# Half of the first mixer's v by seven products of quarters, and the token tiles moved to the front of the constant pool

## The chip, the cores and the metric

The kernel runs on one core of a Trainium2 chip. The metric is the device time of one execution in microseconds (us). The kernel before took 1327.69 us, the median of three runs from 1327.13 to 1328.07.

## The reference

A trunk of two layers works on 512 tokens of width 1024. Layer 0 mixes tokens with a gated MLP (mixer A), layer 1 with a gated linear recurrence (mixer B); after each mixer comes a gated feed-forward part with a short causal convolution (conv_ffn). The change touches mixer A, and within it v:

```
def mixer_a(h, w_in, v_gain, w_s, b_s, w_out):
    z = jax.nn.gelu(h @ w_in)
    u, v = jnp.split(z, 2, axis=-1)
    v = rms_norm(v, v_gain)
    v = v.reshape(bsz, s // CHUNK, CHUNK, A_GROUPS, A_GDIM)
    ws = jnp.tril(w_s).astype(v.dtype)
    sv = jnp.einsum("gts,bcsgd->bctgd", ws, v) + b_s.T.astype(v.dtype)[:, :, None]
    y = u * sv.reshape(bsz, s, A_WIDTH)
    return y @ w_out
```

Here h is the RMS-normed input (512 x 1024), w_in is 1024 x 4096, and u and v are 512 x 2048 each. All inputs and outputs are float32.

## The kernel before

**Numbers in two parts.** Each float32 operand of a product is split into a float32r part hi (a copy by ACT, ScalarE) and a rest lo (a subtraction on DVE, VectorE). A product of two operands is three matmuls: hi by hi, and the two mixed ones. `split` (L95) does this for weights that `load` (L103) brings in on SP's DMA queue; raw, hi and lo tiles rotate in the pool wp through three buffers each.

**Tokens.** `xall` holds the residual stream with the 512 tokens along the free axis, in 8 rows of 512 for the 1024 channels. `norm_input` (L210) writes gain times x in two parts, `xh[k]` and `xl[k]`, 8 tiles of 128 x 512 each. The factor 1/rms of a token, `rc`, is applied to the results instead of to x: as a scale per partition in v, where tokens lie on the partitions, and elsewhere through `rbc`, which is rc spread over all partitions. `norm_stat` (L230) forms sums of squares with eight tiny matmuls (`st`), DVE makes `ms` of them, and a power on POOL (GpSimd) makes `rc` (L226). `norm_spread` (L236) multiplies an identity by the two parts of rc on DVE (tiles `dg`) and sums these over partitions with two matmuls into the bank `rb`, which ACT copies to rbc.

**The constant pool.** `vt` (all gains, biases and convolution taps, 536 columns), `xall`, `xh`, `xl` and, further down, `acc` and `rbc` are declared in this order (L138 to L204), and the pool lays its tiles out in the order of declaration. In the built program the pool begins at byte 16512 of a partition, which is 258 x 64, and vt with it; vt takes 536 x 4 = 2144 bytes, 33.5 x 64, so every tile from xall to xl[7] starts 32 bytes past a multiple of 64. All tiles of the pools wp, yp and y, which hold the other matmul operands, start on a multiple of 64.

**The order of stages.** v in four blocks of 512 features (L359 to L390); u in four blocks, with the spatial product `gate_spatial` (matmuls `sv`) of the block before hooked in between; the output projection `ao`; conv_ffn(0); mixer B (`bx`, gates `gt`, `bg`, projection `bo`); conv_ffn(1). In v the token parts are the stationary operand and the weights (512 columns) the moving one. In u, bx, bg and the up-projections `f` the weights are stationary and xh or xl, 512 columns, moves. In ao, bo, gt and the down-projections xh and xl are not used.

**v, block by block.** Block 0 (`first_chunk`, L344) loads tokens and weights together. Each block has four chunks `kc` of two channel rows each, a chunk being 2 x 4 x 3 matmuls of 512 columns into four PSUM banks; at the end ACT takes each bank through gelu with the scale rc (`vr`) and a square with a running sum (`junk`). norm_stat stands behind block 0, norm_spread in front of chunk 2 of block 1. Afterwards the gain `rv` comes from the sums by the same power on POOL, and `vh` and `vl` (ACT, DVE) are the two parts of the normed v.

**Seven products.** conv_ffn's down-projections use a scheme that multiplies two 2 x 2 arrangements of quarters with seven products in place of eight (`PRODUCTS`, L467; `weight_sums`, L470; `seven`, L510). weight_sums loads three quarters and copies with three DMAs on SP, adds the fourth quarter to two of them with one accumulating DMA on POOL's queue (L475), and leaves two more sums to DVE. seven keeps seven PSUM banks, one for each product; each product of a pair of channel rows is 2 x 3 matmuls of 256 columns.

**Who sets the order.** A scheduler orders the instructions of each engine when the program is built; parts written under `tc.high_priority` come as early as it thinks they can run. On the chip each engine and each DMA queue works through its own list in that order.

Of the kernel before, what the change touches and what calls it, by code (L numbers as in the profile page):

```python
# [44 lines left out]
def trunk(ctx: ExitStack, tc: tile.TileContext, xT, vecs, a_w_in, a_w_sT, a_b_s, a_w_out,  # L45
# [7 lines left out]
    def psum(name="ps"):  # L53
        return pp.tile([P, S], F32, tag="ps", name=name)
# [16 lines left out]
    def keep(tag, name, dt=F32):  # L71
        return phase["yp"].tile([P, S], dt, tag=tag, name=name)
# [18 lines left out]
    def small(n, name):  # L91
        return const.tile([P, n], F32, name=name)
# [10 lines left out]
    def load(shape, parts, name):  # L103
        raw = wp.tile(shape, F32, tag="raw", name=f"{name}r")
        for sl, src in parts:
            nc.sync.dma_start(sl(raw), src)
        return split(raw, shape, name)
# [27 lines left out]
        return f  # L135


    vt = const.tile([P, NV], F32, name="vt")  # L138
    xall = const.tile([P, KD, S], F32, name="xall")
    xs = [xall[:, k, :] for k in range(KD)]  # L140
    xh = [const.tile([P, S], F32R, name=f"xh{k}") for k in range(KD)]
    xl = [const.tile([P, S], F32R, name=f"xl{k}") for k in range(KD)]
    xparts = list(zip(xh, xl))
    g0 = const.tile([P, KD], F32, name="g0")
    nc.scalar.dma_start(g0, vecs[:, _COLS["norm_mix"]:_COLS["norm_mix"] + KD])

    def load_x(k):
        nc.sync.dma_start(xs[k], xT[k * P:(k + 1) * P, :])

    mixer = enter(("yp", 24), ("wk", 6), ("bs", 1))  # L150
    bs = phase["bs"].tile([P, AG, P], F32, name="bs")


# [46 lines left out]
        nc.vector.tensor_scalar(c4, u, LRU_C / 2, None, op0=ALU.mult)  # L200


    acc = const.tile([P, S], F32, name="acc")
    rbc = const.tile([P, S], F32, name="rbc")  # L204
    rc = small(NC, "rc")
    ms = small(NC, "ms")
    rch = const.tile([P, NC], F32R, name="rch")
# [61 lines left out]
    def project_out(kt, w, acts, name):  # L269
# [64 lines left out]
            dg = stat(1)  # L334
        leave(1, dg)

    tiny = small(1, "tiny")
    nc.vector.memset(tiny, 0.0)
    nc.scalar.activation(tiny, tiny, AF.Gelu_apprx_tanh)
# [19 lines left out]
    for fb in range(4):  # L359
        pss = [psum(f"v{c}") for c in range(NC)]  # L360
        for kc in range(KD // 2):
            c0 = AW + fb * 512
            if fb == 0:
                hi, lo = first_chunk(kc, wv[:, 2 * kc:2 * kc + 2, c0:c0 + 512])
            else:
                hi, lo = load([P, 2, 512], [(lambda t: t, wv[:, 2 * kc:2 * kc + 2, c0:c0 + 512])], f"av{fb}{kc}")
            if fb == 1 and kc == 2:
                norm_spread()
            last = kc == KD // 2 - 1
            order = [(k, c) for c in range(NC) for k in range(2)] if last else [(k, c) for k in range(2) for c in range(NC)]  # L370
            for k, c in order:
                kk = 2 * kc + k
                ts = slice(c * P, (c + 1) * P)
                nc.tensor.matmul(pss[c], xh[kk][:, ts], hi[:, k, :], start=kk == 0, stop=False)  # L374
                nc.tensor.matmul(pss[c], xh[kk][:, ts], lo[:, k, :], start=False, stop=False)  # L375
                nc.tensor.matmul(pss[c], xl[kk][:, ts], hi[:, k, :], start=False, stop=kk == KD - 1)  # L376
            if fb == 0:
                square(2 * kc)
# [86 lines left out]
    HS = S // 2  # L465

    PRODUCTS = ((1, 0, 0, 0), (2, 0, 2, 1), (4, 0, 1, 6), (6, 1, 2, 5), (7, 1, 0, 4), (5, 1, 1, 3), (3, 1, 3, 2))  # L467


    def weight_sums(src, name):  # L470
        raw = wp.tile([P, 5, 256], F32, tag="raw", name=f"{name}r")
        for k, n, to in ((1, 0, raw[:, 1:5:3]), (0, 1, raw[:, 0:4:3])):
            nc.sync.dma_start(to, src[:, k, n:n + 1].broadcast_to([P, 2, 256]))
        nc.sync.dma_start(raw[:, 2], src[:, 1, 1])
        nc.gpsimd.dma_start(raw[:, 3:5], src[:, 0, 0:1].broadcast_to([P, 2, 256]), accum_op=ALU.add)  # L475
        sums = phase["sm"].tile([P, 2, 256], F32, tag="sm", name=f"{name}s")

        def part(n, t):
            return tuple(wp.tile([P, n, 256], F32R, tag=g, name=f"{name}{t}{g}", padded_shape=[P, 4, 256]) for g in ("hi", "lo"))

        def fill(hi, lo, src):
            nc.scalar.copy(hi, src)
            nc.vector.tensor_tensor(lo, src, hi.bitcast(F32), op=ALU.subtract)

        with tc.high_priority(HIGH):
            ah, al = part(3, "a")
            fill(ah, al, raw[:, 0:3])
            nc.vector.tensor_tensor(sums[:, 0], raw[:, 0], raw[:, 4], op=ALU.add)
            nc.vector.tensor_tensor(sums[:, 1], raw[:, 2], sums[:, 0], op=ALU.add)
            bh, bl = part(4, "b")  # L490
            fill(bh[:, 0:2], bl[:, 0:2], raw[:, 3:5])
            fill(bh[:, 2:4], bl[:, 2:4], sums)
        return (ah, al), (bh, bl)


    def input_sums(raw, dst):
        nc.vector.tensor_tensor(raw[:, 3:5], raw[:, 0:3:2], raw[:, 7:8].broadcast_to([P, 2, HS]), op=ALU.subtract)  # L497
        nc.vector.tensor_tensor(raw[:, 5], raw[:, 3], raw[:, 2], op=ALU.add)
        nc.vector.tensor_tensor(raw[:, 6], raw[:, 5], raw[:, 1], op=ALU.subtract)  # L499
        hi, lo = dst[:, :, 0:HS], dst[:, :, HS:S]  # L500
        nc.scalar.copy(hi, raw[:, 0:7])  # L501
        nc.vector.tensor_tensor(lo, raw[:, 0:7], hi.bitcast(F32), op=ALU.subtract)  # L502


    def places(raw):
        return raw[:, 0:8:7], raw[:, 1:3]

    def halves(t):
        return t.rearrange("p (h t) -> p h t", h=2)


    def seven(pairs, weight, name):
        banks = {p[0]: psum(f"{name}m{p[0]}").rearrange("p (j t) -> p j t", j=2) for p in PRODUCTS}
        for n, (q, x) in enumerate(pairs):
            parts = weight_sums(weight(q), f"{name}{q}")
            first, last = n == 0, n == len(pairs) - 1
            for b, part, w, i in PRODUCTS:
                hi, lo = parts[part]
                for j in range(2):
                    js = slice(j * P, (j + 1) * P)  # L520
                    for m, (wt, xt) in enumerate(((lo, x[:, i, 0:HS]), (hi, x[:, i, 0:HS]), (hi, x[:, i, HS:S]))):
                        nc.tensor.matmul(banks[b][:, j], wt[:, w, js], xt, start=first and j == 0 and m == 0,  # L522
                                         stop=last and j == 1 and m == 2, skip_group_check=True)
        return banks

    def conv_ffn(l, gain_name, gain_off, chunks):
        stack = enter(("y", 6), ("yr", 1), ("sm", 1), ("wk", 8))
# [240 lines left out]
```

## Time and profile before

| | us |
|---|---|
| median of 3 runs | 1327.69 |
| the profiled execution | 1328.25 |
| its span, first to last instruction | 1326.5 |
| TensorE busy | 1316.4 (99%) |
| VectorE (DVE) busy | 935.2 (71%) |
| ScalarE (ACT) busy | 600.6 (45%) |
| GpSimd (POOL) busy | 54.3 (4%) |

The profile is of one execution. A busy share of 99% tells that matmuls follow each other without a break, and not that each is as short as it could be, since their recorded spans overlap: a matmul of 512 columns is recorded with 0.39 to 0.40 us while the next begins 0.23 us later. The distance from one start to the next is what to read.

### The profile page before, as it was taken

The page shows a single profiled execution, that of the slowest core. Times are in us where ns is not written, and L with a number is a line of the kernel's source. Part 1 is how long each engine was busy: PE and PEld are TensorE (multiplying, and loading weights), DVE is VectorE, ACT ScalarE, POOL GpSimd, SP SyncE. Part 2 cuts the span into 40 slices and gives each one's busy share as a digit, 9 for nine tenths or more (in the row PEclk, how much of TensorE's full clock was granted, in tenths as well). Part 3 has the DMA queues.
Part 4 walks back from the last instruction along what each step waited for, and adds up shares of the span by engine and source line. Part 5 has one row for each costly group of instructions (what it writes and reads, how often), then busy time and mean ns, then how long its engine had stood idle before and what let it go on. Part 6 is the DMA issues. An engine that isn't in the chain of part 4 may idle for free.

```text
span 1326.5 us, 17029 instructions
## 1 busy us (share of the span) xinstructions
PE 1316.4 (99%) x6510; PEld 1103.5 (83%) x6510; DVE 935.2 (71%) x1336; ACT 600.6 (45%) x809; POOL 54.3 (4%) x56
## 2 busy tenths in 40 slices
PE   9999999999999999999999999999999999999997
PEld 7888888888888898888997888888888899888886
DVE  7227776446777877878987799954687788576735
ACT  6456333333444443444554669633344444343432
POOL 1000000000000120001200000000000012000000
PEclk9999999999999999999999999999999999999999
DMA  6333222232223574225752323233222357322221
GB/s 231 96 95 111 81 80 80 95 97 95 95 96 94 124 188 130 89 92 130 178 137 96 96 80 95 96 111 96 84 91 96 111 135 182 113 95 96 96 80 64
DMA packets 121105, 143.47 MB, mean 108 GB/s; under 512 B 7616, under 2 KB 95168, under 8 KB 121024
## 3 DMA queue, kind: packets, MB, share of 16 engines
q1 hardware_dynamic: 111088, 132.95, 31.5%
q0 software_dynamic: 9792, 9.44, 4.7%
q8 instruction: 51, 0.84, 0.3%
q14 instruction: 30, 0.25, 0.1%
q10 hardware_dynamic: 144, 0.00, 0.0%
HBM read 140.26 MB, written 2.10 MB: 107 GB/s over the span
## 4 chain that ended last, share of the span: by engine, by line
PE 99%; issue 1%; DVE 0%; DVEq 0%; POOLq 0%; POOL 0%
PE f L111 14%; PE f L112 14%; PE f L113 14%; PE v L374 2%; PE d000m L522 2%; PE d001m L522 2%; PE v L375 2%; PE u L111 2%; PE d101m L522 2%; PE d061m L522 2%; PE d100m L522 2%; PE d060m L522 2%; PE u L113 2%; PE u L112 2%; PE v L376 2%; PE aop L111 2%
## 5 line engine op out<-in xcount | busy, mean ns | idle before, releaser
L458 DVE SCALAR_TENSOR_TENSOR cv<-up,vt,cv 128x511 f32<-128x511 f32 x192 | 135.8, 745 | 0.7
L545 DVE TENSOR_TENSOR up<-f,rbc 128x512 f32<-128x512 f32 x96 | 63.7, 686 | 35.6 <-PE f L113 33.2
L456 ACT ACTIVATE cv<-up,vt 128x512 f32<-128x512 f32 x96 | 70.7, 804 | 0.5 <-DVE up L545 0.5
L561 ACT ACTIVATE cv<-cv 128x512 f32<-128x512 f32 x48 | 30.3, 632 | 34.4 <-DVE cv L458 34.3
L502 DVE TENSOR_TENSOR y<-yr,y 128x1792 fp32r<-128x1792 f32 x18 | 36.5, 2025 | 11.8 <-ACT y L501 11.8
L501 ACT CAST y<-yr 128x1792 fp32r<-128x1792 f32 x18 | 30.4, 1691 | 14.3 <-DVE yr L499 14.3
L226 POOL TENSOR_TENSOR rc<-ms,mhalf 128x4 f32<-128x4 f32 (+1 forms) x6 | 5.5, 912 | 665.2 <-DVE ms L225 665.2
L434 DVE SCALAR_TENSOR_TENSOR sv<-sv,vt,bs 128x256 f32<-128x256 f32 x32 | 15.0, 478 | 19.1 <-PE sv L431 19.1
L211 ACT ACTIVATE xh<-xall,vt 128x512 fp32r<-128x512 f32 x24 | 17.1, 717 | 20.3 <-DVE xall L263 15.8
L220 ACT ACTIVATE sq<-xall 128x512 f32<-128x512 f32 (+1 forms) x37 | 21.5, 586 | 9.8 <-DVE xall L275 9.8
L563 DVE TENSOR_TENSOR yr<-cv 128x512 f32<-128x512 f32 x36 | 24.7, 688 | 1.7
L458 DVE SCALAR_TENSOR_TENSOR xb<-xr,vt,xb 128x511 f32<-128x511 f32 (+2 forms) x36 | 25.5, 744 | 0.1
L221 DVE TENSOR_TENSOR acc<-acc,sq 128x512 f32<-128x512 f32 (+1 forms) x37 | 23.8, 642 | 2.0 <-ACT sq L220 1.9
L212 DVE SCALAR_TENSOR_TENSOR xl<-xall,vt,xh 128x512 fp32r<-128x512 f32 x24 | 17.8, 747 | 3.4 <-ACT xh L211 3.2
L430 PE MATMUL sv<-ws,vh 128*128 128x256 f32 x64 | 15.4, 324 | 0.0
L436 DVE SCALAR_TENSOR_TENSOR sv<-sv,vt 128x256 f32<-128x256 f32 x32 | 15.0, 479 | 0.4
L567 ACT CAST y<-cv 128x512 fp32r<-128x512 f32 x12 | 7.3, 617 | 16.1 <-DVE cv L565 16.1
L431 PE MATMUL sv<-ws,vl 128*128 128x128 f32 x64 | 14.2, 223 | 0.0
L698 DVE TENSOR_TENSOR_SCAN hs<-riyh,sq 128x512 f32<-128x512 f32 x12 | 14.0, 1207 | 0.0
L86 ACT ACT_TABLE_LOAD x10 | 12.8, 1283 | 0.1
L497 DVE TENSOR_TENSOR yr<-yr 128x512 f32<-128x512 f32 x18 | 12.5, 692 | 0.6
L431 PEld LDWEIGHTS sv<-ws,vl 128*128 128x128 f32 x64 | 12.3, 192 | 0.5
(2631 smaller groups left out, 4505.7 us busy)
## 6 DMA issues: line engine op xcount, KB each, us to landing
xall<-xT SPq DMA_DIRECT2D x8, 256.0 KB, 5.3
outT<-o SPq DMA_DIRECT2D x8, 256.0 KB, 2.2
av00raw<-a_w_in SPq DMA_DIRECT2D x2, 256.0 KB, 4.3
av01raw<-a_w_in SPq DMA_DIRECT2D x2, 256.0 KB, 5.6
av02raw<-a_w_in SPq DMA_DIRECT2D x2, 256.0 KB, 5.8
av03raw<-a_w_in SPq DMA_DIRECT2D x2, 256.0 KB, 4.8
bs<-a_b_s SPq DMA_DIRECT2D x1, 512.0 KB, 5.9
av10r<-a_w_in SPq DMA_DIRECT2D x1, 512.0 KB, 6.0
```

The source lines that it names most:

```text
L111: nc.tensor.matmul(ps, wh, xh, start=first, stop=False)
L112: nc.tensor.matmul(ps, wh, xl, start=False, stop=False)
L113: nc.tensor.matmul(ps, wl, xh, start=False, stop=last)
L374: nc.tensor.matmul(pss[c], xh[kk][:, ts], hi[:, k, :], start=kk == 0, stop=False)
L375: nc.tensor.matmul(pss[c], xh[kk][:, ts], lo[:, k, :], start=False, stop=False)
L456: nc.scalar.activation(dst, src, AF.Identity, scale=col(wname, woff + last * wstep), bias=col(cname, coff))
L458: nc.vector.scalar_tensor_tensor(dst[:, i:], src[:, :S - i], col(wname, woff + (last - i) * wstep), dst[:, i:], op0=ALU.mult, op1=ALU.add)
L501: nc.scalar.copy(hi, raw[:, 0:7])
L502: nc.vector.tensor_tensor(lo, raw[:, 0:7], hi.bitcast(F32), op=ALU.subtract)
L522: nc.tensor.matmul(banks[b][:, j], wt[:, w, js], xt, start=first and j == 0 and m == 0, stop=last and j == 1 and m == 2, skip_group_check= ...
L545: nc.vector.tensor_tensor(upt, pss[2 * half + j], rbc, op=ALU.mult)
L561: nc.scalar.activation(ts[0], ts[0], AF.Gelu_apprx_tanh)
```

## The change

Two edits.

1. In the constant pool the tiles are declared in the order xall, xh, xl, acc, rbc, vt. In the built program xall then begins at byte 16512, and every xh, xl, acc and rbc on a multiple of 64. The pool's size and the places of the other pools are the same.
2. Blocks 2 and 3 of v go by seven products. During block 1 `v_sums` builds, for each pair q of channel rows, the four sums of token halves that the scheme needs (ACT scales two rows into `xg`, four half-width operations on DVE, and the two parts `xq` of the results by ACT and DVE). In blocks 2 and 3 the weights come by `weight_sums`; the seven banks are combined by two copies on ACT and eleven operations on DVE into vr, and gelu and square then read vr. The mixer's work pool (`wk`) has five tiles in place of six; the sixth becomes the tile of weight sums (`sm`).

```diff
-    vt = const.tile([P, NV], F32, name="vt")
     xall = const.tile([P, KD, S], F32, name="xall")
...
     xparts = list(zip(xh, xl))
+    acc = const.tile([P, S], F32, name="acc")
+    rbc = const.tile([P, S], F32, name="rbc")
+    vt = const.tile([P, NV], F32, name="vt")
...
-    mixer = enter(("yp", 24), ("wk", 6), ("bs", 1))
+    mixer = enter(("yp", 24), ("sm", 1), ("wk", 5), ("bs", 1))
...
+    def v_sums(q):
+        g = []
+        for k in (2 * q, 2 * q + 1):
+            t = work(f"xg{k}")
+            nc.scalar.activation(t, xs[k], AF.Copy, scale=g0[:, k:k + 1])
+            g.append((t[:, 0:HS], t[:, HS:S]))
+        (p_, q_), (r_, s_) = g
+        a, b = work(f"xa{q}"), work(f"xb{q}")
+        nc.vector.tensor_tensor(a[:, 0:HS], p_, q_, op=ALU.subtract)
+        nc.vector.tensor_tensor(a[:, HS:S], s_, q_, op=ALU.subtract)
+        nc.vector.tensor_tensor(b[:, 0:HS], a[:, 0:HS], s_, op=ALU.add)
+        nc.vector.tensor_tensor(b[:, HS:S], b[:, 0:HS], r_, op=ALU.subtract)
+        parts = [to_parts(t, f"xq{q}{i}") for i, t in enumerate((a, b))]
...
-    for fb in range(4):
+    for fb in range(2):
...
             if fb == 0:
                 square(2 * kc)
                 square(2 * kc + 1)
+            else:
+                v_sums(kc)
...
+    for fb in range(2, 4):
+        banks = seven_banks(f"v{fb}")
+        for q in range(KD // 2):
+            parts = weight_sums(wv4[:, 2 * q:2 * q + 2, fb], f"av{fb}{q}")
+            for b, part, w, i in PRODUCTS:
+                wh, wl = (t[:, w] for t in parts[part])
+                sh, sl = xsums[q][i]
+                for j in range(2):
+                    js = slice(j * P, (j + 1) * P)
+                    for n, (st, mv) in enumerate(((sh, wh), (sl, wh), (sh, wl))):
+                        nc.tensor.matmul(banks[b][:, j], st[:, js], mv, start=q == 0 and j == 0 and n == 0,
+                                         stop=q == KD // 2 - 1 and j == 1 and n == 2, skip_group_check=True)
+        for c in range(NC):
+            vraw[c, fb] = keep("yl", f"vr{c}{fb}")
+        e1, e5, u2, u3 = (work(f"v{fb}{t}").rearrange("p (j t) -> p j t", j=2) for t in ("e1", "e5", "u2", "u3"))
...
+        for c in range(NC):
+            v_gelu(c, fb, vraw[c, fb])
```

`weight_sums` and `PRODUCTS` are those of the down-projections, moved up in the file unchanged.

How the instructions stand on three engines around block 1 of v. On POOL, around the power that makes rc (`ms` is its input, `av20r` the raw weights of the first pair of block 2), before:

```order
L188 TENSOR_TENSOR lu_121<-ebase_118,nabs_119 128x12
L226 TENSOR_TENSOR rc_128<-ms_129,mhalf_116 128x4
L409 AFFINE_SELECT wsm_844<-wsr_842 128x256
L409 AFFINE_SELECT wsm_849<-wsr_842 128x256
L409 AFFINE_SELECT wsm_854<-wsr_842 128x256
```

and in the change:

```order
L191 TENSOR_TENSOR lu_126<-ebase_123,nabs_124 128x12
L351 DMA av20r_575<-a_w_in 128x2x256
L227 TENSOR_TENSOR rc_131<-ms_132,mhalf_121 128x4
L351 DMA av21r_635<-a_w_in 128x2x256
L351 DMA av22r_695<-a_w_in 128x2x256
```

The first of eight accumulating DMAs now stands ahead of the power; it waits for two of the three loads of av20r on SP's queue.

On DVE, from the parts of rc (rch, rcl) to the tiles dg that norm_spread's matmuls read, before:

```order
L238 TENSOR_TENSOR rcl_131<-rc_128,rch_130 128x4
L100 TENSOR_TENSOR av12l_410<-av12r_407,av12h_409 128x1024
L242 TENSOR_TENSOR dg_416<-ident_111,rch_130 128x512
L242 TENSOR_TENSOR dg_419<-ident_111,rcl_131 128x512
L100 TENSOR_TENSOR av13l_450<-av13r_447,av13h_449 128x1024
```

and in the change, the last twelve of eighteen rows that stand from rch on:

```order
L439 TENSOR_TENSOR xa0_384<-xg1_382,xg0_380 128x256
L440 TENSOR_TENSOR xb0_385<-xa0_384,xg1_382 128x256
L441 TENSOR_TENSOR xb0_385<-xb0_385,xg1_382 128x256
L255 TENSOR_TENSOR xq00l_391<-xa0_384,xq00h_390 128x512
L255 TENSOR_TENSOR xq01l_395<-xb0_385,xq01h_394 128x512
L438 TENSOR_TENSOR xa1_432<-xg2_428 128x256
L439 TENSOR_TENSOR xa1_432<-xg3_430,xg2_428 128x256
L440 TENSOR_TENSOR xb1_433<-xa1_432,xg3_430 128x256
L359 TENSOR_TENSOR av20alo_582<-av20r_575,av20ahi_581 128x768
L441 TENSOR_TENSOR xb1_433<-xb1_433,xg3_430 128x256
L255 TENSOR_TENSOR xq10l_439<-xa1_432,xq10h_438 128x512
L243 TENSOR_TENSOR dg_455<-ident_116,rch_133 128x512
```

Chunk 3's split (av13l), the sums of two pairs and a split of block 2 now stand ahead of the first dg; the second dg follows one row later, behind xq11l.

On TensorE, where the two matmuls of norm_spread (`rb`) stand in block 1, before:

```order
L376 MATMUL v3_346<-av11h_379,xl3_77 128x512
L246 MATMUL rb_415<-dg_416,ones_109 128x512
L246 MATMUL rb_415<-dg_419,ones_109 128x512
L374 MATMUL v0_343<-av12h_409,xh4_70 128x512
L375 MATMUL v0_343<-av12l_410,xh4_70 128x512
```

and in the change:

```order
L470 MATMUL v1_347<-av12l_449,xh5_70 128x512
L247 MATMUL rb_454<-dg_455,ones_114 128x512
L471 MATMUL v1_347<-av12h_448,xl5_78 128x512
L469 MATMUL v2_348<-av12h_448,xh5_70 128x512
L470 MATMUL v2_348<-av12l_449,xh5_70 128x512
L471 MATMUL v2_348<-av12h_448,xl5_78 128x512
L247 MATMUL rb_454<-dg_458,ones_114 128x512
```

They stood in front of chunk 2's 24 matmuls and now stand behind the 17th and the 21st of them.

## Rows read from the trace of the kernel before

**Rows 1.** The page: the chain that ended last, shares of the span by engine.
```profile
PE 99%; issue 1%; DVE 0%; DVEq 0%; POOLq 0%; POOL 0%
```

**Rows 2.** Waits of TensorE, the longest of three: total us, times, longest us.
```profile
PE rb L298 <- DVE dg L291: 1.5, 1, 1.5
```

**Rows 3.** Timeline of TensorE, u to the gates' matmuls, one engine load: start us, us.
```profile
733.64 0.40 PE L113 MATMUL bx<-xh,bx20l 128*128 128x512 f32 x1
...
734.58 0.40 PE L111 MATMUL gt<-xb0h,gw0h 128*128 128x512 f32 x1
...
736.87 0.39 PE L112 MATMUL gt<-xb1l,gw0h 128*128 128x512 f32 x1
```

**Rows 4.** Timeline of TensorE: first matmul of five up blocks, of what follows; same for bop.
```profile
509.08 0.40 PE L111 MATMUL f<-xh,fu070h 128*128 128x512 f32 x1
...
621.53 0.28 PE L522 MATMUL d060m<-y,d0606alo 128*128 128x256 f32 x1
...
851.73 0.40 PE L111 MATMUL bop<-by0h,bow00h 128*128 128x512 f32 x1
...
917.03 0.40 PE L111 MATMUL f<-xh,fu100h 128*128 128x512 f32 x1
```

**Rows 5.** Timeline of TensorE: first matmul of v's block 2, and of u.
```profile
52.65 0.40 PE L374 MATMUL v<-av20h,xh 128*128 128x512 f32 x1
...
97.45 0.40 PE L111 MATMUL u<-xh,au00h 128*128 128x512 f32 x1
```

**Rows 6.** The chain in order of time: seven products of a half, 252 matmuls of 256 columns.
```profile
1075.97 30.23 PE d100m L522 x252
```

**Rows 7.** DMA issues, window 5 to 40 us: size, us to landing.
```profile
vt<-vecs SPq DMA_DIRECT2D x1, 268.0 KB, 5.2
```

**Rows 8.** Timelines of SP and POOL: the load after av11l, and the power that gives rc.
```profile
28.40 0.37 SPq L106 DMA_DIRECT2D av20r<-a_w_in  x1
30.12 1.01 POOL L226 TENSOR_TENSOR rc<-ms,mhalf 128x4 f32<-128x4 f32 x1 [6.85 <-DVE ms L225]
```

**Rows 9.** Timelines of SP and POOL: two sums loaded and added to, d0609r and d0011r.
```profile
619.36 0.88 SPq L473 DMA_DIRECT2D d0609r<-f_w_down  x2
...
623.98 1.20 POOL L475 DMA_DIRECT2D d0609r<-f_w_down  x1 [8.71 <-DMA d0609r<-f_w_down]
...
468.34 0.97 SPq L473 DMA_DIRECT2D d0011r<-f_w_down  x2
...
474.30 1.20 POOL L475 DMA_DIRECT2D d0011r<-f_w_down  x1 [4.18 <-DMA d0011r<-f_w_down]
```

**Rows 10.** Timeline of ACT after rc, in v's second block.
```profile
31.16 1.27 ACT L386 ACTIVATE vr<-v,rc 128x512 f32<-128x512 f32 x2 [1.03 <-POOL rc L226]
...
35.91 1.05 ACT L99 CAST av13h<-av13r 128x1024 fp32r<-128x1024 f32 x1
```

**Rows 11.** Timeline of DVE in the seven products: 256, 768 and 512 elements.
```profile
470.70 0.42 DVE L489 TENSOR_TENSOR d0005s<-d0005r,d0005s 128x256 f32<-128x256 f32 x1
471.04 0.95 DVE L483 TENSOR_TENSOR d0005alo<-d0005r,d0005ahi 128x768 fp32r<-128x768 f32 x1
471.91 0.68 DVE L483 TENSOR_TENSOR d0005blo<-d0005r,d0005bhi 128x512 fp32r<-128x512 f32 x1
```

**Rows 12.** Timeline of TensorE: start of v's second block; spreading of rc.
```profile
29.70 0.48 PE L374 MATMUL v<-av10h,xh 128*128 128x512 f32 x1
...
40.98 0.63 PE L246 MATMUL rb<-dg,ones 128*128 128x512 f32 x2
```

**Rows 13.** Timeline of TensorE from the start: ten bfloat16 matmuls of 512 columns, first of v.
```profile
1.26 4.45 PE L158 MATMUL warm<-warm 128*128 128x512 bf16 x10 [1.26 <-DVE warm L155]
...
5.57 1.73 PE L374 MATMUL v<-av00hi,xh 128*128 128x512 f32 x4
```

**Rows 14.** Timeline of DVE after v: first of u's banks, first sum of sv.
```profile
117.82 1.88 DVE L448 TENSOR_TENSOR u<-u,rbc 128x512 f32<-128x512 f32 x3
...
126.17 0.48 DVE L434 SCALAR_TENSOR_TENSOR sv<-sv,vt,bs 128x256 f32<-128x256 f32 x1 [3.56 <-PE sv L431]
```

More of the change, by code (lines that the diff above doesn't have):

```diff
@@ L200, in log_sigmoid @@
         nc.vector.tensor_scalar(c4, u, LRU_C / 2, None, op0=ALU.mult)
-    acc = const.tile([P, S], F32, name="acc")
-    rbc = const.tile([P, S], F32, name="rbc")
     rc = small(NC, "rc")
@@ L335, in project_out, with weight_sums, part, fill @@
         leave(1, dg)
+    HS = S // 2
+    PRODUCTS = ((1, 0, 0, 0), (2, 0, 2, 1), (4, 0, 1, 6), (6, 1, 2, 5), (7, 1, 0, 4), (5, 1, 1, 3), (3, 1, 3, 2))
+    def weight_sums(src, name):
+        raw = wp.tile([P, 5, 256], F32, tag="raw", name=f"{name}r")
+        for k, n, to in ((1, 0, raw[:, 1:5:3]), (0, 1, raw[:, 0:4:3])):
+            nc.sync.dma_start(to, src[:, k, n:n + 1].broadcast_to([P, 2, 256]))
+        nc.sync.dma_start(raw[:, 2], src[:, 1, 1])
+        nc.gpsimd.dma_start(raw[:, 3:5], src[:, 0, 0:1].broadcast_to([P, 2, 256]), accum_op=ALU.add)
+        sums = phase["sm"].tile([P, 2, 256], F32, tag="sm", name=f"{name}s")
+        def part(n, t):
+            return tuple(wp.tile([P, n, 256], F32R, tag=g, name=f"{name}{t}{g}", padded_shape=[P, 4, 256]) for g in ("hi", "lo"))
+        def fill(hi, lo, src):
+            nc.scalar.copy(hi, src)
+            nc.vector.tensor_tensor(lo, src, hi.bitcast(F32), op=ALU.subtract)
+        with tc.high_priority(HIGH):
+            ah, al = part(3, "a")
+            fill(ah, al, raw[:, 0:3])
+            nc.vector.tensor_tensor(sums[:, 0], raw[:, 0], raw[:, 4], op=ALU.add)
+            nc.vector.tensor_tensor(sums[:, 1], raw[:, 2], sums[:, 0], op=ALU.add)
+            bh, bl = part(4, "b")
+            fill(bh[:, 0:2], bl[:, 0:2], raw[:, 3:5])
+            fill(bh[:, 2:4], bl[:, 2:4], sums)
+        return (ah, al), (bh, bl)
@@ new lines, in input_sums, with places @@
+    def input_sums(raw, dst):
+        nc.vector.tensor_tensor(raw[:, 3:5], raw[:, 0:3:2], raw[:, 7:8].broadcast_to([P, 2, HS]), op=ALU.subtract)
+        nc.vector.tensor_tensor(raw[:, 5], raw[:, 3], raw[:, 2], op=ALU.add)
+        nc.vector.tensor_tensor(raw[:, 6], raw[:, 5], raw[:, 1], op=ALU.subtract)
+        hi, lo = dst[:, :, 0:HS], dst[:, :, HS:S]
+        nc.scalar.copy(hi, raw[:, 0:7])
+        nc.vector.tensor_tensor(lo, raw[:, 0:7], hi.bitcast(F32), op=ALU.subtract)
+    def places(raw):
+        return raw[:, 0:8:7], raw[:, 1:3]
@@ new lines, in halves, with seven_banks, seven @@
+    def halves(t):
+        return t.rearrange("p (h t) -> p h t", h=2)
+    def seven_banks(name):
+        return {p[0]: psum(f"{name}m{p[0]}").rearrange("p (j t) -> p j t", j=2) for p in PRODUCTS}
+    def seven(pairs, weight, name):
+        banks = seven_banks(name)
+        for n, (q, x) in enumerate(pairs):
+            parts = weight_sums(weight(q), f"{name}{q}")
+            first, last = n == 0, n == len(pairs) - 1
+            for b, part, w, i in PRODUCTS:
+                hi, lo = parts[part]
+                for j in range(2):
+                    js = slice(j * P, (j + 1) * P)
+                    for m, (wt, xt) in enumerate(((lo, x[:, i, 0:HS]), (hi, x[:, i, 0:HS]), (hi, x[:, i, HS:S]))):
+                        nc.tensor.matmul(banks[b][:, j], wt[:, w, js], xt, start=first and j == 0 and m == 0,
+                                         stop=last and j == 1 and m == 2, skip_group_check=True)
+        return banks
@@ L357, in first_chunk, with v_gelu @@
         return hi, lo
-    for fb in range(4):
+    xsums = []
+    def v_sums(q):
[11 more added lines that the diff above has]
+        parts = [to_parts(t, f"xq{q}{i}") for i, t in enumerate((a, b))]
+        t0, t1 = slice(0, HS), slice(HS, S)
+        k = 2 * q
+        xsums.append([(h[:, t], l[:, t]) for h, l, t in (
+            (xh[k], xl[k], t0), (xh[k + 1], xl[k + 1], t0), (xh[k + 1], xl[k + 1], t1),
+            (*parts[0], t0), (*parts[0], t1), (*parts[1], t0), (*parts[1], t1))])
+    def v_gelu(c, fb, src):
+        v = vraw[c, fb]
+        nc.scalar.activation(v, src, AF.Gelu_apprx_tanh, scale=rc[:, c:c + 1])
+        junk = work("junk")
+        i = c * 4 + fb
+        nc.scalar.activation(junk, v, AF.Square, accum_out=vsum[:, i:i + 1])
+    for fb in range(2):
         pss = [psum(f"v{c}") for c in range(NC)]
         for kc in range(KD // 2):
[L362 to L366, printed above, removed]
+            src = wv[:, 2 * kc:2 * kc + 2, AW + fb * 512:AW + (fb + 1) * 512]
+            hi, lo = load([P, 2, 512], [(lambda t: t, src)], f"av{fb}{kc}") if fb else first_chunk(kc, src)
             if fb == 1 and kc == 2:
@@ L460, in conv @@
                 op0=ALU.mult, op1=ALU.add)
[L465 to L493, printed above, removed]
@@ L496, in input_sums @@
[L496 to L506, printed above, removed]
@@ L508, in halves @@
[L508 to L524, printed above, removed]
```

27 lines of the change are left out of this document (21 added, 6 removed).

## The prediction

> **What bounds the kernel now.** I read the chain that ended last first. It is TensorE for 99% [rows 1], and the longest wait of that engine is 1.5 us near the end [rows 2]. So in this kernel a microsecond is won or lost only where matmuls start closer together or further apart, or where TensorE newly waits. The next view is therefore TensorE's timeline, read from start to start, since the recorded spans overlap.
>
> There the same shape has two spacings. Five up blocks `f`, 20 x 24 = 480 matmuls of 512 columns, lie between 509.08 and 621.53: 112.45/480 = 0.2343 us each. The 288 of `bop` lie between 851.73 and 917.03: 65.30/288 = 0.2267 [rows 4]. Both have the same tile sizes and the same order of three matmuls. The difference is not one of the stretch either: inside one engine load, the last four matmuls of bx take (734.58 - 733.64)/4 = 0.235, and the ten of gt behind them (736.87 - 734.58)/10 = 0.229 [rows 3]. What sets the two kinds apart is the moving operand. In f, bx, bg and u it is xh or xl, which starts 32 bytes past a multiple of 64, because vt stands ahead of it: its 268.0 KB are 128 rows of 2144 bytes [rows 7], 33.5 times 64. In bop and gt it starts on a multiple. 7.5 ns are 18 columns at 2.4 GHz, close to the 16 float32 values that 64 bytes hold, as if one more piece were read. That is a reading of two numbers, not a proof; no row shows xh at another place.
>
> In v, xh and xl are the stationary operand. From the start of block 2 to u, 44.80 us, lie 192 matmuls: 0.2333 each [rows 5].
>
> **The change, part by part.**
>
> *Starts on 64 bytes, moving operand.* u has 384 such matmuls, the two conv_ffn 2304, bx and bg 288 each: 3264. At 7.5 ns each that is **-24.6 us**. Bounds: nothing, if the spacing has another cause, and these 24.6. I take the whole, since every stage that reads xh has the long spacing and those with other operands the short one. All of it lies on the path as long as the splits of weights keep up; in these stages they stand 6 us or more ahead of their matmuls, and each group of 24 shortens by 0.18 us.
>
> *The same, stationary operand.* Blocks 0 and 1 of v keep 192 matmuls. 0.2333 - 0.2267 = 6.6 ns each: **-1.3 us**, bounds 0 and 1.3.
>
> *Seven products in blocks 2 and 3.* 44.8 us go [rows 5]. In their place come 2 blocks x 4 pairs x 42 = 336 matmuls of 256 columns. 252 of that kind took 30.23 us in the down-projection [rows 6], 0.120 each: 40.3 us. The difference is **-4.5 us**. The weight sums need more loads and more DVE work than a plain split; the down-projection runs two halves of six such pairs with no pause, so eight pairs in a row are covered once the first is ready.
>
> *POOL's queue, and a new wait.* Before, rc is ready at 30.12 + 1.01 = 31.1 [rows 8], and the two matmuls `rb`, at 40.98, find dg done [rows 12]. Now the accumulating DMA of av20r stands ahead of the power, and POOL takes its list in order. That DMA waits for loads that stand behind av11l's on SP, where av20r was issued at 28.40 [rows 8]. In the down-projection POOL began on such a DMA 4.6 us after the first of the two loads was issued (619.36 to 623.98) or 6.0 (468.34 to 474.30), and spent 1.20 on it [rows 9]. So 28.4 + 4.6 + 1.2 = 34.2, and the power ends at 35.2; the ends are 34.3 (loads 0.9 us faster than in the faster of these two) and 36.6.
>
> What is behind rc: ACT has four gelus and four squares, which took from 31.16 to 35.91, and then 1.05 for av13h [rows 10]. DVE waits for that with av13l (1024 wide, about 1.2 by the 768-wide row), and then has the eight small sums of two pairs at 0.42 (256 wide), four parts of 0.68 (512 wide), and av20alo at 0.95 (768 wide) [rows 11], each pair interleaved with ACT's xg and xq. Adding these in the order shown for DVE I get the first dg 13.6 us behind rc, 48.8, and the second at about 50.
>
> TensorE: block 1 starts at 29.70 [rows 12], less 0.5 for the shorter spacing in block 0: 29.2. The first rb now stands behind 65 of its matmuls, 65 x 0.2267 = 14.7: TensorE is there at 43.9. It waits from 43.9 to 48.8: **+4.9 us**, with 3.9 and 6.3 as the ends of rc's range. The four matmuls between the two rb cover most of what the second is late.
>
> *Smaller waits.* In block 2 the bank of the fifth product is free only when the last gelu of block 1 has read it, which now stands behind av21's splits on ACT: +0.35 (0 to 1). The entry into the first seven products of conv_ffn and the rb of bx have thin leads already, and TensorE now comes sooner: +0.4 (0 to 1). u's banks are emptied from 117.82, before the sums of the first `sv` at 126.17 [rows 14]. Now gelu of v's last block reads results that DVE combines first, so the parts of v come some 5.5 us later against TensorE, which was covered by u's first block but for about 0.1. ACT's and DVE's other new work (11 operations a block for the combination) lies beside matmuls.
>
> *Sum:* -24.6 - 1.3 - 4.5 + 4.9 + 0.35 + 0.4 + 0.1 = -24.65. The profiled execution took 1328.25, 0.56 above the median of 1327.69. 1328.25 - 24.65 - 0.56 = **1303.0 us**.
>
> **Rivals.**
>
> *C, the clock falls after the pause.* At the program's start TensorE, idle before, takes 4.45 us for ten matmuls and 1.73 for the first four of v, about 0.43 each; that is 512 columns at the lower level of 1.2 GHz. It is at the upper level some 5.3 us after its first matmul [rows 13]. A pause of nearly 5 us, longer than any in the trace of before, could bring that back: half of 5.3 is lost, about 2.5 us, so 1305.5. Against it: nothing in the rows tells how long a pause may be. The Trainium skill ("TensorE: Matmul & The Clock Gate", What's actually happening) has the idle engine at 1.2 GHz and releases it only after sustained activity; the first matmuls of this trace agree with the second half, and no row of before shows a fall in mid-kernel.
>
> *D, no pause.* The loads land early, or POOL is not held at the accumulating DMA, and ACT and DVE interleave better than I added up: 1303.0 - 4.9 = 1298.1. Against it, POOL shows the wait for such loads as its own idle time [rows 9].
>
> *A, starts on 64 bytes bring nothing.* The spacing would belong to the stage (which pools it reads, how weights follow each other), not to the address. Then -4.5 + 5.75 = +1.25: 1328.9. Against it, the change from 0.235 to 0.229 inside one engine load, where only the operands differ [rows 3]. The Trainium skill speaks for this rival ("TensorE: Matmul & The Clock Gate", Wait — 56ns, not 53.3ns?): it has the distance between matmuls as the number of columns over 2.4 GHz plus a fixed 2.5 ns, about 216 ns for 512 columns, and the address does not occur. By that rule alone both kinds would be equal and the first two terms nothing; the trace, with 226.7 and 234.3 for 512 columns, disagrees on the equality.
>
> *B, slower.* The wait at rb in block 1 outweighs what is won. Place: POOL's queue, av20r's DMA ahead of rc's power. Price: a microsecond for each that rc comes late, plus the clock of C. While starts on 64 bytes count, the wait and what follows from it would have to cost over 30.4 us, which no row comes near. If they don't, the point is lower: 4.5 to make it slower at all, 4.5 + 2.7 = 7.2 to be seen as slower. The wait of 4.9, the small ones of 0.85 and C's 2.5 make 8.25, so +3.75: 1331.4.
>
> **How the numbers follow.** My forecast 0.50, C 0.25, D 0.08, A 0.07, B 0.06; 0.04 is left for what I have not seen, half of it inside the gain. The range goes from 1297.5, a little under D, to 1309.0, which takes in C with the wait at its long end and the small ones at 1 us each, or a fifth of the gain on starts missing: some 0.83 of the chance. A measurement of this kernel can tell about 0.2%, 2.7 us, from no change. The forecast, C, D and half of the rest are faster by more than that, 0.86; A and the other half lie within it or near, 0.08; B is slower, 0.06.
>
> **What would show it.** In the profile of the changed kernel f, u, bx and bg should have a spacing of 0.2267; 0.234 there is rival A. The two blocks from the start of block 2 to u should take 40 to 41 us. POOL should show av20r's DMA at about 33 and rc's power ending at 34 to 37; if rc is at 31, D holds. TensorE should wait at rb for dg, DVE's, at about 44 to 49, the longest wait of the trace, and the matmuls behind it tell by 0.43 or 0.227 between C and the forecast. The prediction is wrong if the wait is over 9 us, if another of over 1 us stands in blocks 2 and 3, or if the spacings don't move.

## The result and the profile after

The changed kernel takes 1313.99 us, the median of four runs (1313.51 to 1315.30), against 1327.76 of the kernel before: a ratio of 0.9898 (95% interval 0.9881 to 0.9916). That is 13.8 us less, where 24.7 were forecast and 1309.0 was the upper end of the range. The profiled execution took 1313.92, its span is 1312.2, 14.3 shorter than before.

TensorE's timeline of the changed kernel (start us, us, engine, line, operation), from v's first matmuls to the first up-projection of layer 1:

```profile
5.59 1.20 PE L469 MATMUL v<-av00hi,xh 128*128 128x512 f32 x4
...
28.90 0.48 PE L469 MATMUL v<-av10h,xh 128*128 128x512 f32 x1
...
43.91 0.40 PE L470 MATMUL v<-av12l,xh 128*128 128x512 f32 x1
48.04 0.77 PE L247 MATMUL rb<-dg,ones 128*128 128x512 f32 x1 [3.73 <-ACT xg L434]
48.60 0.63 PE L471 MATMUL v<-av12h,xl 128*128 128x512 f32 x1
49.03 0.63 PE L469 MATMUL v<-av12h,xh 128*128 128x512 f32 x1
...
53.28 0.41 PE L469 MATMUL v<-av13h,xh 128*128 128x512 f32 x1
...
58.20 0.28 PE L497 MATMUL v2m<-av20ahi,xh 128*128 128x256 f32 x1
...
98.14 0.40 PE L111 MATMUL u<-xh,au00h 128*128 128x512 f32 x1
...
504.27 0.40 PE L111 MATMUL f<-xh,fu070h 128*128 128x512 f32 x1
...
614.15 0.28 PE L401 MATMUL d060m<-y,d0606alo 128*128 128x256 f32 x1
...
843.50 0.40 PE L111 MATMUL bop<-by0h,bow00h 128*128 128x512 f32 x1
...
908.83 0.40 PE L111 MATMUL f<-xh,fu100h 128*128 128x512 f32 x1
```

Read it against [rows 4, 5, 12]. The five up blocks take 614.15 - 504.27 = 109.88 for 480 matmuls, 0.2289 each, where 0.2343 stood before and 0.2267 was expected; bop keeps its 65.33. v's blocks 2 and 3 take 98.14 - 58.20 = 39.94 in place of 44.80. TensorE starts its last matmul before the stop at 43.91, waits there for the tiles dg, and the matmuls behind the stop begin 0.43 apart until 53.28. The granted clock in stretches of 4 us (columns: us, busy time and count of PE, PEld, DVE, ACT, POOL, then PEclk, DMA share, GB/s):

```profile
44.00:48.00 4.00, 0.31 (x2) 0.00 (x0) 4.00 (x9) 3.00 (x6) 1.20 (x1) 0.80 0.31 92
48.00:52.00 4.00, 3.96 (x9) 3.18 (x10) 2.53 (x6) 1.60 (x3) 0.00 (x0) 0.50 0.38 56
52.00:56.00 4.00, 4.00 (x16) 3.21 (x15) 3.09 (x7) 2.99 (x6) 0.00 (x0) 0.84 0.32 86
```

0.50 is the lower level, 1.2 GHz. TensorE's waits (total us, times, longest us); the wait of 1.5 for the last rb, now the second, was the longest before [rows 2]:

```profile
PE rb L247 <- ACT xg L434: 3.7, 1, 3.7
PE rb L299 <- DVE dg L292: 1.5, 1, 1.5
...
PE d060m L401 <- DVE d0607blo L359: 0.6, 1, 0.6
PE d060m L401 <- DVE d06011alo L359: 0.5, 1, 0.5
```

What leads to the first one stands in the timelines of POOL and DVE:

```profile
32.08 1.38 POOL L351 DMA_DIRECT2D av20r<-a_w_in  x1 [9.56 <-DMA av20r<-a_w_in]
33.00 1.55 POOL L227 TENSOR_TENSOR rc<-ms,mhalf 128x4 f32<-128x4 f32 x1
...
36.69 0.43 DVE L364 TENSOR_TENSOR av20s<-av20r 128x256 f32<-128x256 f32 x1 [1.75 <-DMA av20r<-a_w_in]
40.41 1.23 DVE L100 TENSOR_TENSOR av13l<-av13r,av13h 128x1024 fp32r<-128x1024 f32 x1 [2.83 <-ACT av13h L99]
47.21 0.68 DVE L243 TENSOR_TENSOR dg<-ident,rch 128x512 fp32r<-128x512 f32 x1
```

POOL stands idle 9.56 us at the accumulating DMA, rc is ready at 34.55 in place of 31.1 [rows 8], and the first dg ends at 47.89.

Where the 14.3 us of span came from, with sums of start-to-start distances over all matmuls of a stage:

| term | forecast | found | from |
|---|---|---|---|
| starts, moving operand | -24.6 | -16.2 | f 539.9 to 527.7, u 90.4 to 89.0, bx 67.8 to 66.6, bg 67.5 to 66.0 |
| starts, stationary operand | -1.3 | 0 | v's block 1: 0.2333 before and after |
| seven products | -4.5 | -4.9 | 44.80 to 39.94 |
| pause at rb | +4.9 | +3.9 | 48.04 - 43.91, less one distance |
| lower clock behind it | 0 | +2.45 | 12 distances from 48.04 on take 5.24; at 0.2333 they take 2.80 |
| smaller waits | +0.85 | +1.0 | +1.6 in d060m, -0.6 in d000m and d001m |
| v's block 0 | 0 | -0.8 | block 1 starts at 28.90, before at 29.70 |
| rest | 0 | +0.2 | gt 32.84 to 32.99 for the most part |
| sum | -24.65 | -14.35 | |

The gain in block 0 is not one of spacing, which is 0.2333 there too. In the profile of before its first four matmuls took 1.73 us [rows 13], and two start-to-start times near 9 us were 0.40 and 0.34; in this one the four took 1.20, and none behind them is over 0.25. Why the two executions differ there no run shows.

### The profile page after: what moved, and what is told of

Read it like the earlier page. It is cut to its first block, busy times and chain, and to the rows that moved or that the text cites. A ratio compares the mean times of both kernels' runs of the same rounds, so it can differ in the third digit from the quotient of the medians.

```text
span 1312.2 us, 17526 instructions
## 1 busy us (share of the span) xinstructions
PE 1297.4 (99%) x6654; PEld 1106.2 (84%) x6654; DVE 969.1 (74%) x1414; ACT 619.2 (47%) x845; POOL 64.8 (5%) x64
## 4 chain that ended last, share of the span: by engine, by line
PE 93%; DVE 2%; DMA 2%; issue 1%; ACT 1%; DVEq 0%; SPq 0%; POOL 0%; POOLq 0%
PE f L111 13%; PE f L112 13%; PE f L113 13%; PE d101m L401 2%; PE d061m L401 2%; PE d001m L401 2%; PE d000m L401 2%; PE d100m L401 2%; PE u L111 2%; PE u L112 2%; PE u L113 2%; PE aop L111 2%; PE aop L113 2%; PE aop L112 2%; PE bx L113 2%; PE bx L111 2%
## 5 line engine op out<-in xcount | busy, mean ns | idle before, releaser
L627 DVE TENSOR_TENSOR yr<-cv 128x512 f32<-128x512 f32 x36 | 24.7, 688 | 1.7
L577 ACT ACTIVATE u<-u 128x512 f32<-128x512 f32 x16 | 9.4, 624 | 7.1 <-DVE u L576 7.1
```

What stands on the lines that cost most here:

```text
L627: nc.vector.tensor_tensor(places(raw)[j], halves(ts[0]), halves(ts[1]), op=ALU.mult)
```

## Experiments: the two edits apart

The first edit alone, on the kernel before:

```diff
-    vt = const.tile([P, NV], F32, name="vt")
     xall = const.tile([P, KD, S], F32, name="xall")
...
+    acc = const.tile([P, S], F32, name="acc")
+    rbc = const.tile([P, S], F32, name="rbc")
+    vt = const.tile([P, NV], F32, name="vt")
```

> The kernel before with the declaration order of the change and nothing else; the instructions of all engines stand in the same order, only addresses move. Theory of the addresses: the spacings of f, u, bx and bg are those of the changed kernel (sums f 527.7, u 89.0, bx 66.7, bg 66.0 against 539.9, 90.4, 67.8, 67.5 before), so 12.2 + 1.4 + 1.1 + 1.5 = 16.2 us less, of which one or two may come back as a wait at the entry of a down-projection: 1311.5 to 1313.5. Rival, the spacing came from what else the change moved: 1327.8. There is no pause at rb in block 1 in either.

1311.51 us, ratio 0.9885 (0.9870 to 0.9899). In the profiled execution, with 1314.25 the longest of the four, f took 529.8, u 89.0, bx 66.6, bg 66.0; there is no pause at rb. The starts alone bring 16 us, more than the whole change.

The second edit alone, on the changed kernel with vt declared first again:

> The changed kernel with the declaration order of before, so seven products alone; engines' orders as in the changed kernel. Theory: two blocks of v take 39.9 for 44.8 us (-4.9), the pause at rb (+3.9) and the stretch at the lower clock behind it (+2.65) stay, and f, u, bx, bg have their old sums: 1329.0 to 1330.5, that is slower than before. Rival, the pause is the other side of the shorter spacings and is smaller with the long ones: 1326 or less.

1330.2 us, ratio 1.0018 (1.0009 to 1.0028). f is back at 539.9, the pause is 3.8 us and the lower clock follows; d060m waits 1.1 and 0.7. Half of v by seven products costs 2.6 us as it stands, though its matmuls take 4.6 less.

## Experiments: what sets the spacing

If a start on 64 bytes were the whole cause, what is left of 0.2289 above 0.2267 would need another one. The rows were moved against the weights, the order of instructions on every engine staying as it is. First the rows on by 64 bytes:

```diff
+    vsum = small(NC * 4, "vsum")
     xall = const.tile([P, KD, S], F32, name="xall")
...
-    vsum = small(NC * 4, "vsum")
```

> The changed kernel with one 64-byte tile (vsum) declared ahead of the token tiles instead of behind them: xh and xl begin 64 bytes past a multiple of 128, as the weights do, and nothing else moves. Theory A, a start on a multiple of 64 is all that counts: spacings and time as in the changed kernel, 1314. Theory B, streamed operand and weights must start at the same place within 128 bytes: f, u, bx, bg and v's first blocks fall to 0.2268 each, f to 522.5 us, together some 10 us less: 1303.5 to 1306, the upper end if the waits at the entries of the down-projections grow. Theory C, a start at 64 within 128 is short wherever the weights are: the same as B here.

1326.17 us, ratio 0.9987 (0.9978 to 0.9997). f is at 536.8: on multiples of 64, nearly all is lost. This refutes theories A, B and C of the expectation together, since within 128 bytes rows and weights now begin at the same place.

Then the weights and all other operands on by 64, the rows left:

```diff
     vsum = small(NC * 4, "vsum")
+    const.tile([P, 16], F32, name="pad")
```

> The changed kernel with an unused tile of 64 bytes at the end of the constant pool: the tokens' rows stay on a multiple of 128, and the pools of the weights and of all other operands move up by 64 onto multiples of 128. Theory A: 1314. Theory B, same place within 128 bytes: f, u, bx, bg at 0.2268 as in the run before, aop and bop unchanged, 1303.5 to 1306. Theory C, only 64 within 128 is short: f stays at 0.229 and aop, bop, gt and fdp rise to it, some 1100 matmuls by 2.2 ns, 1316.

1307.91 us, ratio 0.9855 (0.9840 to 0.9870): f 522.7, u 87.7, bx 65.7, bg 65.3, all at 0.2267 to 0.2285 us a matmul, aop and bop unchanged. So the period, if there is one, is longer than 128. In addresses, rows minus weights are 160 bytes before, 64 in the changed kernel, 128 and 0 in these two. Three more places, with g0 (32 bytes) declared ahead of xall in the manner of vsum, and with the pad at 128 and at 320 bytes:

```diff
-    const.tile([P, 16], F32, name="pad")
+    const.tile([P, 32], F32, name="pad")
...
+    const.tile([P, 80], F32, name="pad")
```

> The changed kernel with one 32-byte tile (g0) declared ahead of the token tiles: xh and xl begin 96 bytes further on than the weights, counted within 512 bytes, in place of 64 in the changed kernel, 160 in the kernel before, 128 with the rows 64 further on and 0 with the others 64 further on. Theory A, multiples of 64 decide: f at 0.2343, and the time of the seven products alone, 1330. Theory D, the spacing grows with that distance (0.2267, 0.2290, 0.2330, 0.2343 at 0, 64, 128, 160): f between 0.2290 and 0.2330, 1316 to 1325.

> The changed kernel with an unused tile of 128 bytes behind the tokens: the weights now begin 64 bytes further on than xh within 512 bytes (distance -64). Theory D, if only the size of the distance counts: f at 0.2290, 1314 as the changed kernel. If it counts in one direction round a circle of 256 or 512 bytes (192 or 448): f at 0.233 to 0.236, 1326 to 1332. Theory A: 1314.

> The changed kernel with an unused tile of 320 bytes behind the tokens: weights and rows begin 256 bytes apart within 512. Theory D with a circle of 256 bytes: f at 0.2267 and 1308, as with 64 bytes. With a circle of 512 bytes or more: f at 0.233 or longer, 1326 to 1332. Theory A: 1314.

1326.99, 1326.94 and 1309.57 us, one execution each. f is at 537.8, 537.8 and 522.7: a circle of 256 bytes. Two runs then asked for the rule where it says something unlikely. The kernel before, every declaration in its old order, with a pad of 160 bytes behind the tokens, so that neither the rows nor the weights start on a multiple of 64:

```diff
     vsum = small(NC * 4, "vsum")
+    const.tile([P, 40], F32, name="pad")
```

> The kernel before, declarations in its own order, with one unused tile of 160 bytes behind the tokens: xh and xl still start 32 bytes past a multiple of 64, and so now do the weights, at the same place within 256 bytes. Theory of the distance: f 522.7, u 87.7, bx 65.7, bg 65.3, v 87.4, and 1301.6, with no operand on a multiple of 64. Theory A, a start on a multiple of 64 decides: f stays at 539.9, aop, bop, gt and the seven products lengthen too, 1328 or more.

1301.57 us, ratio 0.9803 (0.9787 to 0.9819), f 522.6. And the output projection, which never reads xh, put 128 bytes off its weights, in the version that comes last below (1301.64 us):

```diff
-    mixer = enter(("yp", 24), ("wk", 6), ("bs", 1))
+    mixer = enter(("pd", 1), ("yp", 24), ("wk", 6), ("bs", 1))
+    phase["pd"].tile([P, 32], F32, name="pad2")
```

> The fastest version so far (rows first, the 64-byte tile, no seven products in v; 1301.64) with an unused tile of 128 bytes ahead of mixer A's pools, so that ay, which the output projection aop streams, begins 128 bytes off its weights within 256. Theory of the distance: aop goes from 87.3 to some 89.5 us (384 at 0.2330), bop and f stay at 65.3 and 522.7, the time at 1303.8. Rival, the distance matters for xh and xl alone, for another reason: aop 87.3, 1301.6.

1303.01 us, one execution; aop went from 87.3 to 89.4, bop stayed at 65.3. All places together, as the distance in bytes, moving minus stationary start within 256; in f the rows move, in v the weights do, so the same address counts the other way:

| kernel | f: bytes | f: mean ns | v, block 1: bytes | v: mean ns |
|---|---|---|---|---|
| rows first, others +64 | 0 | 226.9 | 0 | 227.4 |
| rows first, others +320 | 0 | 226.9 | 0 | 227.4 |
| before, others +160 | 0 | 226.8 | 0 | 227.2 |
| the change | 64 | 229.0 | 192 | 233.3 |
| rows +32 | 96 | 233.4 | 160 | 234.3 |
| rows +64 | 128 | 233.0 | 128 | 232.4 |
| before | 160 | 234.3 | 96 | 233.3 |
| others +128 | 192 | 233.4 | 64 | 228.9 |

Both columns tell the same for 512 columns: 0 is best, 64 costs some 2 ns, the rest 5 to 8. Means of f are its sum over 2304; those of v are over the start-to-start times of block 1 ahead of any pause, without the first (0.32 us). The rows behind three of the lines, first and last of five up blocks in TensorE's timeline; rows +64, others +64, and before with others +160:

```profile
509.26 0.39 PE L111 MATMUL f<-xh,fu070h 128*128 128x512 f32 x1
...
620.81 0.28 PE L402 MATMUL d060m<-y,d0606alo 128*128 128x256 f32 x1
```
```profile
501.90 0.40 PE L111 MATMUL f<-xh,fu070h 128*128 128x512 f32 x1
...
610.73 0.28 PE L401 MATMUL d060m<-y,d0606alo 128*128 128x256 f32 x1
```
```profile
498.37 0.40 PE L111 MATMUL f<-xh,fu070h 128*128 128x512 f32 x1
...
607.20 0.28 PE L523 MATMUL d060m<-y,d0606alo 128*128 128x256 f32 x1
```

For 480 matmuls 111.55, 108.83 and 108.83.

For 256 columns the order is another one. The seven products of v show it with the same addresses as block 1; blocks 2 and 3, with others +64 (distance 0) and others +128 (distance 64):

```profile
58.10 0.28 PE L498 MATMUL v2m<-av20ahi,xh 128*128 128x256 f32 x1
...
98.41 0.40 PE L111 MATMUL u<-xh,au00h 128*128 128x512 f32 x1
```
```profile
58.08 0.28 PE L498 MATMUL v2m<-av20ahi,xh 128*128 128x256 f32 x1
...
97.44 0.39 PE L111 MATMUL u<-xh,au00h 128*128 128x512 f32 x1
```

They take 40.31 and 39.36 us. The matmuls among them that read xh or xl start 120 ns apart at distance 0 and 113 at 64, with 117.5 to 119.4 at the other places; those that read xq, which no run moved against the weights, stay at 120. So the best distance for 512 columns is the worst of those seen for 256. The 1512 matmuls of 256 columns in the down-projections take 0.120 each; whether another distance shortens them was not tried.

Why the distance matters inside the chip no run tells.

## Experiments: the pause

POOL's order alone, so that rc doesn't wait for av20r:

```diff
-        nc.gpsimd.dma_start(raw[:, 3:5], ..., accum_op=ALU.add)
+        with tc.issue_after(last_pow[-1].ins):
+            nc.gpsimd.dma_start(raw[:, 3:5], ..., accum_op=ALU.add)
```

> The changed kernel with av20r's accumulating DMA made to stand behind rc's power on POOL; nothing else is asked for. Theory: rc is ready at about 31 in place of 34.5, so the pause at rb shrinks from 3.9 to about 0.4 us, and TensorE stays at the upper clock, which gives back another 2.65: 1313.99 - 3.5 - 2.65 = 1307.8. Rival one, the pause is set by ACT's and DVE's other work ahead of dg: it stays, 1314. Rival two, the pause goes and the lower clock comes at another place: 1310.5.

1313.07 us, ratio 0.9887 (0.9871 to 0.9904), near rival one's 1314 and far from the theory's 1307.8. rc is ready at 30.88, 3.7 earlier, but the wait at rb only falls from 3.7 to 2.2, and the lower clock still follows. Its timelines of POOL and DVE:

```profile
29.87 1.01 POOL L228 TENSOR_TENSOR rc<-ms,mhalf 128x4 f32<-128x4 f32 x1 [6.83 <-DVE ms L227]
32.86 1.37 POOL L353 DMA_DIRECT2D av20r<-a_w_in  x1 [1.98 <-DMA av20r<-a_w_in]
...
38.66 0.43 DVE L366 TENSOR_TENSOR av20s<-av20r 128x256 f32<-128x256 f32 x1 [6.23 <-DMA av20r<-a_w_in]
39.47 1.22 DVE L101 TENSOR_TENSOR av13l<-av13r,av13h 128x1024 fp32r<-128x1024 f32 x1
...
46.26 0.69 DVE L244 TENSOR_TENSOR dg<-ident,rch 128x512 fp32r<-128x512 f32 x1
```

The sum av20s stands ahead of av13l on DVE, and waits 6.23 us for the same DMA to land. The DMA held two queues: POOL's at its start and DVE's at its landing. Freeing one leaves the other.

Then rb itself moved to where nothing waits for it, the third pair of block 3:

```diff
-            if fb == 1 and kc == 2:
-                norm_spread()
...
+            if fb == 3 and q == 2:
+                norm_spread()
             parts = weight_sums(wv4[:, 2 * q:2 * q + 2, fb], f"av{fb}{q}")
```

> The changed kernel with norm_spread (dg and rb) called in front of the third pair of v's block 3 in place of chunk 2 of block 1; the power stays behind av20r's DMA. Theory: TensorE no longer waits at rb in block 1, so the pause (3.9) and the stretch at the lower clock (2.45 beyond its time at the upper level) go; block 2 then starts near 51.4, and its weights and sums, on DVE until about 60 in the changed kernel, are some 2 us late: 1313.99 - 3.9 - 2.45 + 2 = 1309.6, from 1307.5 to 1311.5. Rival, DVE's work decides when block 2 can run wherever rb stands, and the pause only moves to block 2: 1313 to 1314.5.

1315.64 us (1312.54 to 1316.64), ratio 0.9905 (0.9890 to 0.9920): no gain, above the range that was given and above its rival's. The waits of TensorE in the profiled run, the fastest of the four, tell where the pause went; what made the other three 2.5 to 4.1 us longer no trace shows.

```profile
PE v2m L497 <- ACT vr L451: 3.1, 2, 2.3
```

The fifth product of block 2, and after it the seventh, need PSUM banks that gelus of block 1 have yet to read, and ACT got to those gelus late, in part because rc was late (the two runs below). In the changed kernel the pause at rb had hidden this wait. Both edits together with the pad of 64 bytes, and the same without the edit on POOL's order:

> Three edits on the changed kernel: the 64-byte tile behind the tokens (1307.91 alone), norm_spread in v's block 3, and av20r's accumulating DMA behind rc's power. Theory: the tile's gain and the pause's add, the pause being 4.5 there: 1307.9 - 4.4 - 2.9 + 2.5 = 1303, from 1301 to 1306. Rival, as in the run before (DVE decides): 1307 to 1308.5.

> The same without the edit on POOL's order (the power stays behind av20r's DMA). If the landing of that DMA is what DVE waits for in front of chunk 3's split, this is the faster of the two by about 1 us, since the DMA then starts about 1 us earlier: 1302. If rc's lateness is what counts, it is slower by 2 to 3: 1306.

1303.56 (ratio 0.9816, 0.9802 to 0.9831) and 1306.86 (0.9843, 0.9829 to 0.9858). Against the pad alone, 1307.91, the edits give 4.4 together; the wait for vr is 2.2 us, in two pieces, with the power first and 3.4 in one with the power behind the DMA, so rc's lateness counts. Behind the wait of 3.4 the clock falls to the lower level too. Shorter waits went both ways: 2.2 us at rb with the power first (the kernel of 1313.07) was followed by a fall, 2.3 us with rb moved was not. Their stretches, with the 3.4 first:

```profile
56.00:60.00 4.00, 2.97 (x14) 2.97 (x15) 3.18 (x6) 4.00 (x10) 1.10 (x1) 0.66 0.46 73
```
```profile
48.00:52.00 4.00, 4.00 (x14) 3.12 (x13) 1.80 (x6) 1.97 (x4) 0.00 (x0) 0.70 0.17 26
```
```profile
56.00:60.00 4.00, 2.64 (x20) 2.43 (x20) 3.17 (x6) 4.00 (x10) 0.95 (x1) 1.00 0.48 79
```

Last, the kernel before with the first edit and the pad of 64 bytes, so no seven products in v:

> The kernel before with the declaration order of the change and the unused 64-byte tile behind the tokens, and without seven products in v. Theory of the distance within 256 bytes: f 522.7, u 87.7, bx 65.7, bg 65.3 as in the changed kernel with that tile, and all four blocks of v at 0.2275, 2.6 less: 1311.51 - 7.1 - 1.3 - 0.9 - 0.7 - 2.6 = 1298.9, up to 1301 if the down-projections wait at their entry. That would show the seven products in v to be a loss as they stand. Rival, DVE's splits become the bound: 1305 or more.

1301.64 us, ratio 0.9805 (0.9788 to 0.9821), f 522.7, v's four blocks 87.4. With the pad of 160 bytes on the kernel before (1301.57) it is the fastest version found: some 12 us below the change and 26 below the kernel before.

## Why the prediction was wrong, and where it was right

- **Starts, moving operand: mis-sized, and its rule was wrong.** The step said that a start on a multiple of 64 bytes gives the spacing of bop. What counts is the distance between the moving and the stationary operand within 256 bytes. The kernel before has 160, bop 0, the change 64: the step compared the ends and took the change for the far end. 16.2 of 24.6 us came. The lower spacing was to be had, as the pad shows, and rows on a multiple of 64 at a distance of 128 bring next to nothing. The words "that is a reading of two numbers" were right; the range did not act on them, with 0.07 for no effect and little between none and all.
- **Starts, stationary operand: nothing came of 1.3.** The distance went from 96 to 192, both 233.3. With the pad it came (227.4), and in the changed kernel it would only have lengthened the pause, which ends when DVE does.
- **Seven products: right.** 39.94 us for 40.3.
- **The new wait: right in place, near in size, and with half of its cause.** POOL started the DMA at 32.08 (33.0 forecast), rc was ready at 34.55 (35.2), dg 13.3 us behind it (13.6), and the wait was 3.9, where 4.9 was taken between 3.9 and 6.3. Left out was that DVE waits for the DMA's landing too; under the late rc this was nearly covered, 1.75 us, and showed only when rc came early: then 2.2 of the 3.7 stayed.
- **The clock: rival C, given 0.25, is what happened.** 2.45 us where it put 2.5; that the size fits is in part luck, since in the second edit alone the matmuls behind a pause of 3.8 lost 1.6. It follows a pause, not the change's other work: every such stretch in v stands behind a wait of TensorE, of 2.2 to 4.5 us, and the kernels that have only shorter ones there have none. The wait of 2.3 without a fall, beside that of 2.2 with one, shows that the length alone does not decide. The Trainium skill ("TensorE: Matmul & The Clock Gate", What's actually happening) has an idle engine fall to 1.2 GHz, and the trace agrees with 0.50 granted behind the pause of 3.9.
- **Smaller waits: near in sum, 1.0 for 0.85, by luck.** The bank of block 2's fifth product cost nothing, as it lay behind the pause; the wait came in d060m, 1.6 us, and d000m and d001m lost 0.6 that they had before. It is not the earlier arrival of TensorE, since the first edit alone arrives earlier and has none. The timelines of POOL and DVE, first of the changed kernel, then of the first edit alone:

```profile
593.87 1.20 POOL L351 DMA_DIRECT2D d0606r<-f_w_down  x1 [105.28 <-DMA d0606r<-f_w_down]
...
600.03 0.43 DVE L364 TENSOR_TENSOR d0606s<-d0606r 128x256 f32<-128x256 f32 x1 [4.20 <-DMA d0606r<-f_w_down]
```
```profile
592.48 1.19 POOL L475 DMA_DIRECT2D d0606r<-f_w_down  x1 [104.45 <-DVE up L545]
...
597.08 0.43 DVE L488 TENSOR_TENSOR d0606s<-d0606r 128x256 f32<-128x256 f32 x1 [2.19 <-DMA d0606r<-f_w_down]
```

  From issue to use 6.2 us in the one and 4.6 in the other, and DVE, which is full there, passes the delay on. From issue to landing it took 5.2 to 6.2 us in all eleven profiles with seven products in v and 4.0 to 4.8 in the five without; what lengthens it was not tried.
- **Rival A fell.** Addresses alone move the time by 26 us. The Trainium skill ("TensorE: Matmul & The Clock Gate", Wait — 56ns, not 53.3ns?) has the time from one matmul's start to the next depend on the columns and the clock alone; here 512 columns take 226.8 to 234.3 ns by address, and the measurement decides.

With the measured 16.2 for the starts, C's 2.5 and the rest as forecast, the sum is -16.2 - 4.5 + 4.9 + 2.5 + 0.85 = -12.45, and 1315.2 us. The chances add up a little differently from what the prediction says: 0.85 for faster and 0.09 for within reach of no change, in place of 0.86 and 0.08; nothing hangs on it.

## What to carry to other kernels

Read matmul spacing from start to start, and where equal shapes differ, compare the start addresses of both operands, not one of them: here 160 bytes of unused SBUF in front of the weights brought nearly twice what the change did. Which distance is best is to be measured for each shape, since 256 columns had another order than 512. Where one number separates two groups of rows, list everything else that separates them too, and give the values in between a chance. A transfer that waits in an engine's queue can hold two engines, the one that issues it and the one that uses it first; moving one of them, look for the other.

## What was not expected

At a distance of 64 bytes the spacing has two steady forms under the same addresses. In u's first block and the first of bx the start-to-start times lie about 233.3 ns throughout; behind the first interruption (the matmuls of sv in u, of st in bx) they turn to a cycle of 232, 226, 229, mean 229.0, and mostly stay there. It can also stay in the first form for long: in the profile of the first edit alone the last five up blocks of layer 1, and in that of rb moved to block 3 the five of layer 0, lie at 233.3 throughout, which costs 2.1 us each (f 529.8 in place of 527.7). So the same kernel can differ by such steps from one execution to the next. At distance 0 none of the 96 groups of 24 in f went to the long form: apart from one start-to-start time of 0.32 us in two of them, their means are 226.6 to 229.0. What sets the form was not tried.
